# The projection weights of the stick-breaking layer: split in the second FFN stage, kept in DRAM as halves, and loaded as halves

## The chip, the cores and the metric

The kernel runs on one core of one Trainium2 chip. The metric is the device time of one execution in microseconds (us). Engines are called PE (TensorE's matmuls; PEld its weight loads), DVE (VectorE), ACT (ScalarE), POOL (GpSimd) and SP (SyncE, whose queue issues nearly all DMAs).

## The reference

The network runs over 1024 tokens of width 1024, all in float32. In order: an FFN (SwiGLU, 1024 to 2816 to 1024), a token mixer with two kinds of softmax attention, a second FFN, a layer with a linear recurrence and a state-space scan (the even layer, on 1040 tokens: 16 meta tokens are put in front), and the stick-breaking layer (the odd layer), which the change is about:

```python
u = rmsnorm(h, norm_w)
q, k, v, g = jnp.split(u @ w_in, 4, axis=-1)          # w_in: 1024 x 4096
...                                                   # 16 heads of 64
z = einsum(q, k) * 64 ** -0.5
log_keep = where(before, log_sigmoid(-z), 0)
csum = cumsum(log_keep, axis=-1)
weights = where(before, exp(log_sigmoid(z) + csum[..., -1:] - csum), 0)
o = einsum(weights, v)
o = o * silu(g)
return h + o @ w_out
```

## The kernel before

**Exact products from halves.** Every operand of a large product is split into two halves of the type `F32R`: `hi`, a rounding copy made on ACT (`nc.scalar.copy`), and `lo = raw - hi`, made on DVE. A product is three matmuls (`mm3`, lines 336 to 338): hi by hi, hi by lo, lo by hi. Weights come from DRAM as they are ("raw") and are split in SBUF (`Stream.split`, line 473 for the subtraction; the cast has the line of a wrapper, 224).

**Stages.** Five stages follow one another: first FFN, mixer, second FFN, even layer, odd layer. In the profile below they begin at about 0, 640, 1330, 1990 and 2790 us. Inside a stage, the work is written as many small threads (Python generators). Each says before an instruction which engine it needs and how long it will take by the planner's own costs ("A" for ACT, "V" for DVE, "P" for PE, "D" for SP's queue), and waits for buffers (`Res`) and events (`Ev`). The planner `Sched` picks the thread that can start first, and among equals the one of the lower priority number; this sets the order of the instructions. The framework below it places semaphores and buffers, and lets an instruction pass others on its engine when its buffers are free: the first DMA of the thread `ahead_of` (below) leaves at 31.4 us, although the planner starts that thread behind products that PE reaches later.

**Weight units of the odd layer.** `odd_stage` (line 2150) takes the 4096 columns of `w_in` as 32 units of 128 x 1024 numbers (512 KB): for each of eight pairs of heads p one unit for q, k and g each (`Stream.cols`: 128 columns, all eight blocks of 128 rows), and for each two pairs two units for v. Their order is q, k, g, v, v for p = 0, then q, k, g for odd p and q, k, v, v, g for even p; the last is g of pair 7. `Stream.thread` (line 479) loads a unit into one of 2 raw tiles, waits for one of 3 pairs of buffers (`wh`, `wl`) and starts the split. The pair comes free when PE is done with the unit.

**The odd stage's order.** The projections (`proj`) are the lowest in priority and fill PE between the parts of the attention, which goes pair by pair: scores `psc`, two sigmoids on ACT (`kt`, `pt`), a scan on DVE (line 2235), a product on DVE (line 2239), transposes `ptr` on PE (line 1573), their split into `th` on ACT and `tl` on DVE (line 1524), and the matmuls `po` with v (line 1556). The result goes to DRAM (`ooD`). Then comes the output projection (`Attention.out_proj`, line 1638; matmuls `pwo`, lines 1696 to 1698): when the projections are done it loads the halves of `w_out` into the buffers Ah and Al that held the stage's input, and then, block by block of 128 tokens, the operands `or` from `ooD`, into raw tiles:

```python
for k in range(KD):
    for x in range(2):
        yield ("D", 1.6)
        nc.sync.dma_start(WO[x][:, k, :D].bitcast(F32), w_out[x, k])
    ...
for t in range(8):
    yield ready(0, t // 2)
    yield W.r_raw
    yield W.r_hl
    raw = W.raw("o")
```

**Halves made ahead.** For the output weights of the mixer and of the odd layer this is already done: `Stream.ahead_of` (line 507) loads a unit, splits it, and stores both halves to a DRAM tensor (`wo1` in the first FFN stage, `wo2` in the even stage; tiles `pre`, eight units each, both raw tiles for one unit). In an FFN stage the thread `halves_ahead` runs it with the lowest priority from the fourth block of the gate and up weights on. In the second FFN stage it does not run; its two raw tiles hold a meta row and two loads for the even layer.

Of the kernel before, what the change touches and what calls it, by code (L numbers as in the profile page):

```python
# [427 lines left out]

class Stream:
# [4 lines left out]
    def __init__(self, c, eng="V", pool=None, nraw=0, nhl=0, shared=True):  # L434
# [44 lines left out]
    def thread(self, items, prio=4):  # L479

        c = self.c
        for key, units in items:
            if key in self.w:
                continue
            parts = []
            for x, srcs in enumerate(units):
                srcs = srcs if isinstance(srcs, tuple) else (srcs,)
# [12 lines left out]
                t = yield DMA_IN  # L500
                c.sch.spawn(self.split(raw[:, :n], hi[:, :n], lo[:, :n], n,
                                       self.ev[key] if x == len(units) - 1 else None, self.eng), prio, t)
                v = lambda t: t[:, :n].rearrange("p (k f) -> p k f", k=m)
                parts.append((v(hi), v(lo)))
            self.w[key] = lambda k, parts=parts, m=m: (parts[k // m][0][:, k % m], parts[k // m][1][:, k % m])

    def ahead_of(self, w, dst):

        nc = self.c.nc
        for k in range(KD):  # L510
            yield self.r_raw
            yield self.r_raw
            raw, hi = self.raw("pre"), self.raw("pre", F32R)
            yield ("D", 1.6)
            nc.sync.dma_start(raw, w[k * P:k * P + P, :])
            yield DMA_IN
            yield ("A", act(1024))
            nc.scalar.copy(hi, raw)
            yield ("V", dve(1024))
            nc.vector.tensor_sub(raw.bitcast(F32R), raw, hi.bitcast(F32))  # L520
            yield 0.5
            yield ("D", 1.6)
            nc.sync.dma_start(dst[0, k], hi.bitcast(F32))
            yield ("D", 1.6)
            nc.sync.dma_start(dst[1, k], raw)
# [154 lines left out]
def ffn_stage(c, A, first, rows0, wg, wu, wd, gpost, res, rows, nxt, meta=None, cols=None, later=None):  # L680
# [13 lines left out]
    with ExitStack() as ctx:  # L694
# [621 lines left out]
        def halves_ahead():  # L1316
            yield event("prod", 3, 1, "g")
            yield from W.ahead_of(*later)
# [31 lines left out]
class Attention:  # L1350
# [3 lines left out]
    def __init__(self, c, ctx, A, w_in, col0, psb, np_, nth, lo_eng):  # L1354
# [6 lines left out]
        self.W = Stream(c, lo_eng)  # L1361
# [276 lines left out]
    def out_proj(self, oD, w_out, after, ready, evac, last=KD - 1):  # L1638
# [10 lines left out]
        def load():  # L1649
            yield after  # L1650
            WO.extend(c.new_A())
            for k in range(KD):
                for x in range(2):
                    yield ("D", 1.6)
                    nc.sync.dma_start(WO[x][:, k, :D].bitcast(F32), w_out[x, k])
# [78 lines left out]
def mixer_stage(c, A, rows0, prm, w_in, forget_b, lams, subln, rope, w_out, gpost, res, rows):  # L1734
# [3 lines left out]
    with ExitStack() as ctx:  # L1738
        T = Attention(c, ctx, A, w_in, 0, dict(sc=3, tr=2, po=1, mm=2), 6, 2, "V")
# [410 lines left out]
def odd_stage(c, A, rows0, prm, w_in, w_out, res, final, out):  # L2150
# [3 lines left out]
    with ExitStack() as ctx:  # L2154
        T = Attention(c, ctx, A, w_in, M, dict(sc=3, tr=2, po=1, mm=2), 6, 2, "V")
# [5 lines left out]
        order = []  # L2161
        for p in range(8):
            order += [(p, "q"), (p, "k")] + ([(p, "g"), (p, "v")] if p == 0 else [(p, "v"), (p, "g")] if p % 2 == 0
                                             else [(p, "g")])
        items = [(j, Stream.cols(w_in, "qkvg".index(j[1]) * D + j[0] * P, 256 if j[1] == "v" else P)) for j in order]
        for key, _ in items:
            W.expect(key)
# [291 lines left out]
def even_stage(c, A, rows0, prm, w_in, lru_wa, lru_wx, dt_bias, a_log, ssd_d, w_out, meta, res, rows, later):  # L2459
# [701 lines left out]
    def weights():  # L3161
        yield from W2.into(w_out, D, WO[0], WO[1], ev_wl, 2, "V")
        yield from W2.ahead_of(*later)
# [15 lines left out]
def kernel(ctx, tc, x, ffn1_pre_g, ffn1_post_g, ffn1_w_gate, ffn1_w_up, ffn1_w_down, mix_pre_g, mix_post_g,  # L3179
# [19 lines left out]
    wo1, wo2 = (c.dr.tile([2, KD, P, D], F32, name=nm) for nm in ("wo1", "wo2"))  # L3199
# [6 lines left out]
                   later=(w_out[0], wo1))  # L3206
# [7 lines left out]
    def meta_rows(t, junk):  # L3214
# [15 lines left out]
    A4 = even_stage(c, A3, rows3, prm, even_w_in_2[0], lru_w_a_2[0], lru_w_x_2[0], ssd_dt_bias_2,  # L3230
                    ssd_a_log_2, ssd_d_2, even_w_out_2[0], meta_2, x3, rows4, (odd_w_out_2[0], wo2))
    odd_stage(c, A4, rows4, prm, odd_w_in_2[0], wo2, h1,
# [36 lines left out]
```

## Time and profile before

| | |
|---|---|
| median of 3 runs | 3589.42 us (3587.85 to 3590.59) |
| the profiled execution | 3594.18 us, of which span 3592.5 us |
| PE, DVE, ACT, POOL busy | 96%, 77%, 47%, 9% of the span |
| granted PE clock, mean | 0.987 |
| DMA traffic | 366.07 MB, mean 102 GB/s |
| HBM read, written | 267.58 MB, 95.13 MB |

"Busy" is the time in which an engine executes; matmuls are pipelined, so the bars of neighbouring matmuls overlap and the busy time of PE says that it is fed, not that it is at its peak. Times of rows count from the start of the span. `x<-y` names the tile that an instruction writes and those that it reads. "Idle before" is time in which the engine stood still in front of an instruction, with what ended it. A thing on "the chain" is a piece of the path that ended last, followed back from the end.

### The profile page before, as it was taken

To read this page: it belongs to the slowest core of one execution; us is meant where nothing else is said; L and a number is where in the kernel's file an instruction comes from. 1 tells how busy PE (TensorE), PEld (TensorE's weight loads), DVE (VectorE), ACT (ScalarE), POOL (GpSimd) and SP (SyncE) were. 2 spreads that over 40 slices of the span, in tenths; PEclk is the share of its full clock that TensorE was granted. 3 is DMA by queue.
4 is the path that set the end of the run, shared out by engine and by line. 5 is a ranking of instruction groups with operands and counts; after the bars stand their busy time and mean duration, and the time that the engine had idled before them with its cause. 6 is when DMAs were issued, how large, how long until landed. Compare 5 with 4: busy or idle time off the path is not lost.

```text
span 3592.5 us, 51852 instructions
## 1 busy us (share of the span) xinstructions
PE 3434.7 (96%) x19675; PEld 2929.4 (82%) x19675; DVE 2763.9 (77%) x5074; ACT 1696.3 (47%) x3451; POOL 328.0 (9%) x355
## 2 busy tenths in 40 slices
PE   8899999899999999999999899998999999999998
PEld 6688888778888877888888899988878888888877
DVE  8877689988888769766799779578633788788784
ACT  4333244556666543233345447447422565556551
POOL 0111144000000001111351000000000000000000
PEclk9999999999999999999999999999999999999999
DMA  5452382321211551323562334244473110111133
GB/s 168 146 174 91 103 289 86 123 61 44 67 43 39 178 167 61 122 88 108 178 212 67 111 63 86 61 87 89 139 241 94 57 36 22 39 30 30 34 134 107
DMA packets 305842, 366.07 MB, mean 102 GB/s; under 512 B 18644, under 2 KB 221568, under 8 KB 305592
## 3 DMA queue, kind: packets, MB, share of 16 engines
q1 hardware_dynamic: 299800, 341.71, 30.6%
q10 hardware_dynamic: 5792, 21.04, 1.6%
q8 instruction: 155, 2.54, 0.3%
q14 instruction: 95, 0.78, 0.1%
HBM read 267.58 MB, written 95.13 MB: 101 GB/s over the span
## 4 chain that ended last, share of the span: by engine, by line
PE 71%; DVE 19%; ACT 5%; issue 3%; DMA 2%; SPq 0%; POOL 0%; ACTq 0%; DVEq 0%; POOLq 0%
PE pst L338 7%; PE pst L337 7%; PE pst L336 7%; PE po L1556 3%; PE pe L336 3%; PE pe L338 3%; PE pe L337 3%; DVE kt L2235 3%; PE pdn L337 2%; PE pdn L338 2%; PE pdn L336 2%; PE ptr L1573 2%; DVE dl L1073 2%; PE pwo L3060 2%; PE pwo L3061 2%
## 5 line engine op out<-in xcount | busy, mean ns | idle before, releaser
L336 PE MATMUL pe<-Ah,wh 128*128 128x260 f32 (+1 forms) x1184 | 341.2, 289 | 19.9 <-DVE sz L2561 7.9
L338 PE MATMUL pe<-Ah,wl 128*128 128x260 f32 (+1 forms) x1184 | 337.8, 286 | 0.0
L337 PE MATMUL pe<-Al,wh 128*128 128x260 f32 (+1 forms) x1184 | 337.1, 285 | 0.0
L224 ACT CAST wh<-w 128x512 fp32r<-128x512 f32 x280 | 161.8, 619 | 225.3 <-PE pst L337 137.8
L338 PE MATMUL pst<-Ah,wl 128*128 128x512 f32 x640 | 253.3, 397 | 11.8 <-DVE wl L473 11.8
L916 DVE TENSOR_TENSOR sg<-sg,pst 128x512 f32<-128x512 f32 x280 | 185.9, 680 | 98.4 <-PE pst L338 98.1
L980 POOL TENSOR_TENSOR h<-h 128x512 f32<-128x512 f32 x88 | 137.2, 1560 | 1339.4 <-DVE h L962 1334.3
L337 PE MATMUL pst<-Al,wh 128*128 128x512 f32 x640 | 255.1, 399 | 0.0
L336 PE MATMUL pst<-Ah,wh 128*128 128x512 f32 x640 | 253.9, 397 | 1.2 <-DVE sg L916 1.2
L1524 DVE TENSOR_TENSOR tl<-ptr,th 128x512 fp32r<-128x512 f32 (+2 forms) x344 | 198.6, 591 | 63.9 <-ACT th L224 61.2
L473 DVE TENSOR_TENSOR wl<-w,wh 128x512 fp32r<-128x512 f32 x280 | 211.6, 782 | 44.7 <-ACT wh L224 43.4
L336 PEld LDWEIGHTS pe<-Ah,wh 128*128 128x128 f32 (+1 forms) x1184 | 224.1, 189 | 24.3 <-DVE sz L2561 8.2
L224 ACT CAST th<-ptr 128x512 fp32r<-128x512 f32 (+2 forms) x344 | 171.2, 515 | 147.2 <-PE ptr L1573 137.7
L337 PE MATMUL pdn<-dl,dh 128*128 128x512 f32 x592 | 230.8, 390 | 2.3 <-DVE dl L1073 2.3
L338 PE MATMUL pdn<-dh,dl 128*128 128x512 f32 x592 | 230.3, 389 | 0.0
L336 PE MATMUL pdn<-dh 128*128 128x512 f32 x592 | 229.0, 389 | 0.0
L337 PEld LDWEIGHTS pe<-Al,wh 128*128 128x128 f32 (+1 forms) x1184 | 223.6, 189 | 1.0
L338 PEld LDWEIGHTS pe<-Ah,wl 128*128 128x128 f32 (+1 forms) x1184 | 223.5, 189 | 0.8
L2235 DVE TENSOR_TENSOR_SCAN kt<-kt,onec 128x392 f32<-128x392 f32 (+6 forms) x224 | 202.5, 913 | 25.4 <-ACT kt L224 24.1
L224 ACT CAST wh<-wr 128x1024 fp32r<-128x1024 f32 (+2 forms) x116 | 119.3, 1028 | 167.8 <-PE pwo L3061 75.9
L336 PE MATMUL pst<-T,wh 128*128 128x512 f32 x480 | 187.6, 391 | 2.8 <-ACT T L224 2.8
L338 PE MATMUL pst<-T,wl 128*128 128x512 f32 x480 | 186.7, 390 | 1.1 <-DVE wl L473 1.1
(552 smaller groups left out, 10103.4 us busy)
## 6 DMA issues: line engine op xcount, KB each, us to landing
hD<-h SPq DMA_DIRECT2D x22, 1792.0 KB, 6.2
w<-in_ffn_w_gate_dram SPq DMA_DIRECT2D x20, 1024.0 KB, 5.5
w<-in_ffn_w_up_dram SPq DMA_DIRECT2D x20, 1024.0 KB, 7.8
d<-hD SPq DMA_DIRECT2D x18, 1024.0 KB, 5.5
wr<-in_even_w_in_dram SPq DMA_DIRECT2D x36, 512.0 KB, 4.6
wo<-prer SPq DMA_DIRECT2D x32, 512.0 KB, 3.2
wr<-in_odd_w_in_dram SPq DMA_DIRECT2D x32, 512.0 KB, 4.2
wr<-in_w_in_dram SPq DMA_DIRECT2D x24, 512.0 KB, 3.9
```

What stands on the lines that cost most here:

```text
L224: self.last = _o(*a, **k)
L336: nc.tensor.matmul(ps, wh, xh, start=start, stop=False)
L337: nc.tensor.matmul(ps, wh, xl, start=False, stop=False)
L338: nc.tensor.matmul(ps, wl, xh, start=False, stop=stop)
L473: (nc.gpsimd if eng == "G" else nc.vector).tensor_sub(lo, raw, hi.bitcast(F32))
L916: nc.vector.tensor_add(dst, src, ps)
L980: nc.gpsimd.tensor_sub(q[:, o], q[:, a], q[:, b_])
L1073: nc.vector.tensor_sub(lo, v[:, r], hi.bitcast(F32))
L1524: nc.vector.tensor_sub(tl[:rows, :n], ptr[:rows, :n], th[:rows, :n].bitcast(F32))
L1556: nc.tensor.matmul(po[:, 256 - n:256], vs, (th, tl)[which][:rows, o:o + n], start=(x == 0 and y == 0), stop=(x == last and y == len(lhs) - 1))
L1573: nc.tensor.transpose(ptr[:rows, o:o + P], pts[i][:, col:col + rows], c.ident)
L2235: nc.vector.tensor_tensor_scan(rev, rev, c.one.to_broadcast([P, m]), kt[:, k0 + m:k0 + m + 1], op0=ALU.mult, op1=ALU.mult)
```

## The change

The second FFN stage gets a list of 32 units to make ahead (`later=odd_u`): it loads each unit of the odd layer's `w_in` in the layout in which the odd stage will use it, casts it on ACT, subtracts on DVE, and stores both halves to a DRAM tensor `wio` (32 units, two halves each, 32 MB). The odd stage loads both halves of a unit by two DMAs, directly into a pair (`wh`, `wl`), and casts and subtracts nothing. Its two raw tiles become a fourth pair, until the projections are done; then `give_raw` returns them to the output projection. The output weights use the same class `Halves`, with no change in what is done for them.

```diff
+class Halves:
+    def __init__(self, src, dst):
+        self.src, self.dst, self.shape = src, dst, src.shape
+        self.n = src.shape[1] * src.shape[2]
+    @staticmethod
+    def of(c, name, items):
+        n = sum(len(us) for _, us in items)
+        dst = c.dr.tile([n, 2, P, 1024], F32, name=name)
...
 class Stream:
+        if halves:
+            self.hls.append((None, 0))
-        self.r_raw, self.r_hl = Res(len(self.raws)), Res(len(self.hls))
+        self.r_raw, self.r_hl = Res(0 if halves else len(self.raws)), Res(len(self.hls))
...
     def hl(self, name):
         pool, n = self.hls[self.ihl % len(self.hls)]
         self.ihl += 1
+        if pool is None:
+            return self.raw(name, F32R), self.raw(name, F32R)
...
+    def give_raw(self):
+        if self.hls[-1][0] is None:
+            yield self.r_hl
+            self.hls.pop()
+            for _ in range(len(self.raws)):
+                self.r_raw.release(self.c.sch.time)
...
     def thread(self, items, prio=4):
+                if isinstance(srcs, Halves):
+                    m, n = srcs.shape[1], srcs.n
+                    yield self.r_hl
+                    hl = [h[:, :n] for h in self.hl("w")]
+                    for y, h in enumerate(hl):
+                        t = yield ("D", 0.2 + 1.4e-3 * n)
+                        c.nc.sync.dma_start(h.bitcast(F32), srcs.dst[y, :, :n])
...
-    def ahead_of(self, w, dst):
+    def ahead_of(self, units):
-        for k in range(KD):
+        for u in units:
+            n = u.n
             yield self.r_raw
             yield self.r_raw
-            raw, hi = self.raw("pre"), self.raw("pre", F32R)
+            raw, hi = self.raw("pre")[:, :n], self.raw("pre", F32R)[:, :n]
-            nc.sync.dma_start(raw, w[k * P:k * P + P, :])
+            nc.sync.dma_start(raw.rearrange("p (k f) -> p k f", k=u.shape[1]), u.src)
             yield DMA_IN
             nc.scalar.copy(hi, raw)
             nc.vector.tensor_sub(raw.bitcast(F32R), raw, hi.bitcast(F32))
             yield 0.5
-            nc.sync.dma_start(dst[0, k], hi.bitcast(F32))
-            nc.sync.dma_start(dst[1, k], raw)
+            for x, h in enumerate((hi.bitcast(F32), raw)):
+                yield ("D", 0.2 + 1.4e-3 * n)
+                nc.sync.dma_start(u.dst[x, :, :n], h)
...
     def out_proj(self, oD, w_out, after, ready, evac, last=KD - 1):
             yield after
+            yield from W.give_raw()
             WO.extend(c.new_A())
...
+    odd, odd_u = Halves.of(c, "wio", odd_weights(odd_w_in_2[0]))
     A3 = ffn_stage(c, A2, False, rows2, ffn2_w_gate[0], ffn2_w_up[0], ffn2_w_down[0], ffn2_post_g, x2,
-                   rows3, even_weights(even_w_in_2[0], lru_w_a_2[0], lru_w_x_2[0])[:NXT], meta_rows)
+                   rows3, even_weights(even_w_in_2[0], lru_w_a_2[0], lru_w_x_2[0])[:NXT], meta_rows,
+                   later=odd_u)
```

## Rows read from the trace of the kernel before

**Rows 1.** The page: busy time, share of the span and instructions of each engine.
```profile
PE 3434.7 (96%) x19675; PEld 2929.4 (82%) x19675; DVE 2763.9 (77%) x5074; ACT 1696.3 (47%) x3451; POOL 328.0 (9%) x355
```

**Rows 2.** Busy time by stretch (stretch, length, then each engine), odd stage.
```profile
2780.00:3440.00 660.00, 618.23 (x4200) 547.32 (x4199) 518.01 (x914) 374.51 (x901) 16.97 (x132) 0.99 0.12 35
```

**Rows 3.** Line 1556, 2830 to 3440 us: what ended its idle time (us, times).
```profile
  DVE tl L1524: 70.9, 84
```

**Rows 4.** The chain, 2780 to 3440 us: start, us, what.
```profile
2787.58 1.05 ACT wh L224
...
2820.14 1.20 DVE wl L473
...
3339.79 1.06 ACT wh L224
3340.87 1.23 DVE wl L473
```

**Rows 5.** Busy time by stretch, first and second FFN stage (PE, PEld, DVE, ACT, POOL, clock, DMA).
```profile
138.00:212.00 74.00, 74.00 (x323) 60.46 (x322) 59.74 (x90) 27.77 (x46) 10.44 (x5) 1.00 0.61 215
...
1375.00:1450.00 75.00, 69.89 (x298) 55.55 (x297) 71.58 (x107) 25.11 (x44) 12.89 (x8) 0.98 0.31 102
1450.00:1550.00 100.00, 100.00 (x436) 81.62 (x436) 69.12 (x106) 31.25 (x56) 17.80 (x12) 1.00 0.29 98
```

**Rows 6.** Tile wr, 2800 us to the end: ns min/median/max, first and last start.
```profile
L224 ACT CAST wh<-wr x29: 1042/1049/1137, 2818.6 to 3408.0; 128x1024 fp32r<-128x1024 f32 x29
L473 DVE TENSOR_TENSOR wl<-wr,wh x29: 1189/1216/1226, 2820.1 to 3409.1; 128x1024 fp32r<-128x1024 f32 x29
```

**Rows 7.** DMA issues of the whole kernel: count, KB each, median us to landing.
```profile
wr<-in_odd_w_in_dram SPq DMA_DIRECT2D x32, 512.0 KB, 4.2
...
Al<-wo SPq DMA_DIRECT2D x16, 512.0 KB, 10.7
```

**Rows 8.** Waits of SP's queue, 2740 us to the end: total, times, longest.
```profile
SPq L496 <- DVE wl L473: 339.7, 25, 42.6
```

**Rows 9.** Timeline of SP's queue at the end of the odd stage: start, us, instruction.
```profile
3407.23 3.51 SPq L1674 DMA_DIRECT2D or<-ooD  x2
...
3463.48 0.32 SPq L1655 DMA_DIRECT2D Ah<-wo  x1
...
3483.33 0.39 SPq L1674 DMA_DIRECT2D or<-ooD  x1
```

**Rows 10.** Tile pg (gates), 3400 us to the end: the last matmul's start.
```profile
L338 PE MATMUL pg<-Ah,wl x28: 389/394/400, 3400.2 to 3463.0; 128*128 128x512 f32 x28
```

**Rows 11.** Tile pwo (output projection), 3440 us to the end: first and last start.
```profile
L1696 PE MATMUL pwo<-Ah,oh x128: 387/394/477, 3469.6 to 3582.4; 128*128 128x512 f32 x128
```

**Rows 12.** Busy time by stretch, instructions on tile pwo alone.
```profile
3464.00:3495.00 31.00, 10.32 (x36) 6.31 (x36) 0.00 (x0) 0.00 (x0) 1.00 0.79 292
```

**Rows 13.** Busy time by stretch, all instructions, the end of the odd stage.
```profile
3464.00:3495.00 31.00, 27.62 (x162) 20.82 (x161) 30.24 (x53) 19.20 (x48) 0.49 (x5) 1.00 0.79 292
3495.00:3584.00 89.00, 88.29 (x412) 72.16 (x412) 47.81 (x133) 19.87 (x37) 0.00 (x0) 1.00 0.34 110
```

**Rows 14.** Tile prer (units made ahead), 130 to 215 us: ns min/median/max.
```profile
L520 DVE TENSOR_TENSOR prer<-prer x7: 1210/1224/1226, 138.7 to 209.1; 128x1024 fp32r<-128x1024 f32 x7
...
L224 ACT CAST prer<-prer x6: 1048/1053/1055, 144.6 to 207.4; 128x1024 fp32r<-128x1024 f32 x6
```

**Rows 15.** Timeline of SP's queue, 138 to 216 us: loads of units made ahead.
```profile
140.41 0.38 SPq L515 DMA_DIRECT2D prer<-in_w_out_dram  x1
...
187.23 1.66 SPq L515 DMA_DIRECT2D prer<-in_w_out_dram  x1
...
203.03 0.37 SPq L515 DMA_DIRECT2D prer<-in_w_out_dram  x1
```

**Rows 16.** Timeline of SP's queue, 1285 to 1400 us: a raw tile is taken again.
```profile
1385.39 0.37 SPq L496 DMA_DIRECT2D wr<-in_even_w_in_dram  x1
```

**Rows 17.** Busy time by stretch, the down projection of the second FFN stage.
```profile
1770.00:1981.00 211.00, 209.82 (x925) 172.98 (x923) 203.40 (x266) 107.90 (x197) 79.00 (x37) 1.00 0.49 169
```

More of the change, by code (lines that the diff above doesn't have):

```diff
@@ L426, with place, __init__ @@
 DMA_IN = 2.4
+class Halves:
[6 more added lines that the diff above has]
+        dst = c.dr.tile([n, 2, P, 1024], F32, name=name)
+        units = []
+        def place(u):
+            units.append(Halves(u, dst[len(units)]))
+            return units[-1]
+        return [(key, [place(u) for u in us]) for key, us in items], units
 class Stream:
     RAW, HL = 2, 3
-    def __init__(self, c, eng="V", pool=None, nraw=0, nhl=0, shared=True):
+    def __init__(self, c, eng="V", pool=None, nraw=0, nhl=0, shared=True, halves=False):
         self.c, self.eng = c, eng
@@ L486, in thread @@
             for x, srcs in enumerate(units):
+                if isinstance(srcs, Halves):
[5 more added lines that the diff above has]
+                        c.nc.sync.dma_start(h.bitcast(F32), srcs.dst[y, :, :n])
+                    if x == len(units) - 1:
+                        self.ev[key].set(t + DMA_IN)
+                    parts.append([h.rearrange("p (k f) -> p k f", k=m) for h in hl])
+                    continue
                 srcs = srcs if isinstance(srcs, tuple) else (srcs,)
@@ L1317, in halves_ahead @@
             yield event("prod", 3, 1, "g")
-            yield from W.ahead_of(*later)
+            yield from W.ahead_of(later)
         def begin():
@@ L1350, with __init__ @@
 class Attention:
-    def __init__(self, c, ctx, A, w_in, col0, psb, np_, nth, lo_eng):
+    def __init__(self, c, ctx, A, w_in, col0, psb, np_, nth, lo_eng, halves):
         self.c, self.A, self.w_in, self.col0 = c, A, w_in, col0
@@ L1360, in __init__ @@
         self.pq, self.pv, self.pp, self.pm = opn("aQ"), opn("aV"), opn("aP"), opn("aM")
-        self.W = Stream(c, lo_eng)
+        self.W = Stream(c, lo_eng, halves=halves)
         self.np, self.nth = np_, nth
@@ L2145, in mixer_stage, with odd_weights, odd_stage @@
     return nA[0]
-def odd_stage(c, A, rows0, prm, w_in, w_out, res, final, out):
+def odd_weights(w_in):
+    order = []
+    for p in range(8):
+        order += [(p, "q"), (p, "k")] + ([(p, "g"), (p, "v")] if p == 0 else [(p, "v"), (p, "g")] if p % 2 == 0
+                                         else [(p, "g")])
+    return [(j, Stream.cols(w_in, "qkvg".index(j[1]) * D + j[0] * P, 256 if j[1] == "v" else P)) for j in order]
+def odd_stage(c, A, rows0, prm, w_in, items, w_out, res, final, out):
     nc, tc, sch = c.nc, c.tc, c.sch
@@ L2154, in odd_stage @@
     with ExitStack() as ctx:
-        T = Attention(c, ctx, A, w_in, M, dict(sc=3, tr=2, po=1, mm=2), 6, 2, "V")
+        T = Attention(c, ctx, A, w_in, M, dict(sc=3, tr=2, po=1, mm=2), 6, 2, "V", True)
         T.identb = prm["identb"]
@@ L2160, in odd_stage @@
         gts = {}
[L2161 to L2166, printed above, removed]
+        order = [key for key, _ in items]
+        for key in order:
             W.expect(key)
@@ L3162, in weights @@
         yield from W2.into(w_out, D, WO[0], WO[1], ev_wl, 2, "V")
-        yield from W2.ahead_of(*later)
+        yield from W2.ahead_of(later)
     sch.spawn(weights(), 2)
@@ L3197 @@
     x1, x2, x3, h1 = (rows_of(nm) for nm in ("x1", "x2", "x3", "h1"))
-    wo1, wo2 = (c.dr.tile([2, KD, P, D], F32, name=nm) for nm in ("wo1", "wo2"))
+    rows_w = lambda w: [("o", [w.rearrange("(k p) f -> p k f", p=P)[:, k:k + 1] for k in range(KD)])]
+    wo1, wo2 = (Halves.of(c, nm, rows_w(w))[1] for nm, w in (("wo1", w_out[0]), ("wo2", odd_w_out_2[0])))
     A = c.new_A()
@@ L3205 @@
                    x[0], rows1, mixer_weights(w_in[0])[:NXT], cols=cols,
-                   later=(w_out[0], wo1))
+                   later=wo1)
     rows2 = Rows(c, prm["g2"], x2, 0, 0)
```

16 lines of the change are left out of this document (7 added, 9 removed).

## The prediction

> **What bounds the kernel now.** I began with the page's busy line: TensorE (PE) is busy for 96% of the span, VectorE (DVE) for 77% [rows 1]. That is a mean over five stages, so next came the table of busy time by stretch for the last stage, the stick-breaking layer, whose weights the change moves. From 2780 to 3440 us PE is busy 618.2 of 660 us, DVE 518.0 and ScalarE (ACT) 374.5 [rows 2]: 41.8 us are left in which PE does nothing. The answer for line 1556 says what it waits for: weight loads and matmuls of that line sat 70.9 us, in 84 waits, for `tl`, a DVE result [rows 3] (a wait of a weight load and of its matmul overlap, so this counts parts twice). So the stage is a PE stage with holes, and the holes are DVE's. The chain of waits shows which DVE work is ahead of them: among its longest pieces from 2780 to 3440 us stand six casts `wh` on ACT (first at 2787.58, last at 3339.79) and eleven subtractions `wl` on DVE (first at 2820.14, last at 3340.87) [rows 4]. These are the splits of the projection weights.
>
> The second FFN stage, which gets the work, looks different: between 1450 and 1550 us PE is busy all 100 us, DVE only 69.1 and ACT 31.3 [rows 5].
>
> **The change part by part.** *Removed from the last stage:* 32 casts and 32 subtractions, one of each per weight unit. 29 of them fall behind 2800 us, at a median of 1.049 us and 1.216 us [rows 6]; 32 x 1.05 = 34 us of ACT, 32 x 1.22 = 39 us of DVE. What counts is the part on the path: 11 x 1.2 + 6 x 1.05 = 13.1 + 6.3 = 19.4 us [rows 4]. That is the most this chain can give. The least is nothing: the next chain, through the scans and `tl` themselves, may end just as late. I take half, 10 us: six of the eleven subtractions stand alone on the chain (some 7 us that only push other DVE work back), while five come as a pair behind a cast that itself waited for PE to free a buffer, and there a part of the wait stays.
>
> The Trainium skill would have this at nothing: "Perfetto Trace Analysis", section "Identifying the Most-Contended Engine", says in my words that the engine with the highest occupancy is the one to relieve, and that is PE here. By that rule this term is 0 and the sum is 10 us higher; it is weighed with the rivals.
>
> *Loads in place of splits.* Each unit now needs two 512 KB loads where it had one, straight into the buffers that the matmuls read. A raw load landed in 4.2 us (median), low halves of `wo`, loaded in bursts of sixteen, in 10.7 us [rows 7]; the split took 1.05 + 1.22 us with its load done beforehand. So a unit is ready some 2 to 8 us later after a buffer comes free. Against that stands a fourth pair of buffers (the two raw tiles). The first q, k and g of the stage use buffers that PE frees one after another before it needs them. I cost this at 0, for behind 2800 us no DMA is among the long pieces of the chain; without that cover it would be those 2 to 8 us for each unit that PE reaches early. SP's queue waits for these loads already: 339.7 us in all, 25 times, for a subtraction to free a raw tile [rows 8]; now it waits for PE to free a buffer. Behind them in the queue stand the `ooD` stores, and DVE's join of two heads waits for the two buffers that they free; one kind of wait in that queue takes the place of another of the same number, so I cost this at 0 too.
>
> *The end of the last stage.* The last weight unit (gate columns of head pair 7) is number 32 of 32, and 32 is a multiple of four, so it lies in the raw pair. Before, both raw tiles were free early: the first loads of the output projection's operands, `or<-ooD`, left at 3407.23 us [rows 9]. Now they can leave only when the last gate matmul is done, which starts at 3463.0 us [rows 10]. At that moment the 16 loads of the output weights `Ah/Al<-wo` become free to go too (from 3463.48), and they stand ahead in the order of the stage; the next `or` load behind them left at 3483.33 [rows 9]. SP's queue holds these, and behind them the later `or` loads and the `ooD` stores. So I expect the first operand to be loaded behind 8 MB, split by about 3495 us, and the matmuls `pwo`, which started at 3469.6 us [rows 11], to start some 25 us later. In 3464 to 3495 us they are 36 matmuls and 10.3 us of PE's busy time [rows 12]; at 100 / 436 = 0.23 us a matmul, as where PE is never idle [rows 5], that is 8.3 us. PE cannot fill the hole with attention, since DVE is busy 30.2 of these 31 us, nor catch up, since from 3495 us on it is busy 88.3 of 89 us [rows 13]. Cost: 0 (if the operands still come first) to 10.3 us; I take 8, the row it is nearest to being the 36 matmuls at their spacing.
>
> *Added to the second FFN stage:* 32 units of load, cast, subtraction and two stores. The first FFN stage has eight such units for the first output weights, so their price can be read: a cast takes 1.05, a subtraction 1.22 us [rows 14]. Six of them lie in 138 to 212 us, where DVE rises to 59.7 of 74 us (81%) and the DMA engines to 61%, and PE is still busy 74.00 of 74.00 us [rows 5]. So one unit in about 12 us costs PE nothing there. 32 of them add 39 us of DVE and 48 MB of traffic to a stage that has 31% of DVE free while it makes gate and up. SP's queue gets 96 more DMAs; behind their waits stand the loads of gate and up weights, as in the first stage, where PE saw nothing of it.
>
> The question is whether they are done in time. Two raw tiles allow one unit at once. From load to load the first stage took (203.03 - 140.41) / 5 = 12.5 us, at most 15.8 [rows 15]. The raw tiles are both free from 1385.39 us [rows 16], and the down projection begins at about 1770 us; 32 x 12.5 = 400 us ends at 1786 us, one or two units late. In the down projection DVE is busy 203.4 of 211 us [rows 17], so a unit there costs up to its 1.22 us. I take 1 us (two units less what the free 7.6 us swallow); bounds 0, and 7.7 units x 1.22 = 9.4 us at the slowest spacing.
>
> **Sum.** -10 + 8 + 1 = -1 us. Against the profiled execution's own 3594.18 us (span 3592.5 and 1.7 around it) that is 3593.2; this execution stands 4.8 us above the median of 3589.42, so the forecast is 3588 us: no change that can be measured. A change within 0.2% (7.2 us) is what a measurement of this kernel cannot tell from none.
>
> **Rivals.**
> *Faster: the holes close.* If the whole 19.4 us of splits come off the chain and the new order of the stage loads the first `or` operands early enough for half of the 8 us, the sum is -19.4 + 4 + 1 = -14: 3575 us. For it: PE's 41.8 us of holes are twice that, and they follow DVE. Against it: scans and `tl`, not the splits, are most of DVE's time there.
>
> *Slower: the late output projection alone decides.* Its place is 3464 to 3495 us, its price 8.3 to 10.3 us. If the relief of DVE gives less than about 2 us, because PE's own work sets the stage (it is busy 94% of it [rows 2]) and another DVE operation is late in the place of `wl`, the sum is 0 + 9 + 1 = +10: 3599 us. The rule of the Trainium skill named above leads to this case; the 70.9 us of waits for `tl` speak against it.
>
> *Slower: the units reach the down projection.* At 15.8 us each they end at 1385 + 506 = 1891 us; 7.7 units lie behind 1770 us, in front of `dl`, the operand that PE waits for there. With the other terms as forecast: -10 + 8 + 9.4 = +7.4, or 3597 us. It decides from a spacing of about 13 us on. For it: DVE is nearly full from 1375 to 1450 us (71.6 of 75 [rows 5]), so the first units may be slow. Against it: the trace shows idle DVE and ACT to fill.
>
> **How the numbers follow.** No measurable change 0.42, the holes close 0.32, the output projection alone 0.14, spill 0.12. Both slower cases lie above 7.2 us, so faster 0.32, same 0.42, slower 0.26. The range takes the faster case in, down to the bounds of -19.4 + 0 + 1 (3571), and both slower ones with some of what lies above them: 3571 to 3602 us. The likeliest case alone reaches from 3582 to 3596.
>
> **What would show it.** Right: no `wl<-wr` or `wh<-wr` behind the last even-layer operand; PE's busy time in the last stage up to `pwo` shorter by some 10 us for the same matmuls; the first `or<-ooD` load behind the last gate matmul and `pwo` starting 30 us behind it instead of 7; PE in the second FFN stage still at 100% until the down projection, with 32 subtractions `pre` at 1.2 us about 12 us apart. Wrong: the wait of line 1556 for `tl` unchanged (the term of -10), an `or` load ahead of the `wo` loads (the +8), `pre` operations behind 1800 us or holes of PE beside gate and up weights (the +1), or a wait of PE for a load from the new DRAM tensor (the 0).

## The result and the profile after

The changed kernel takes 3670.13 us (median of 4 runs, 3663.43 to 3673.99) against 3589.72 us: ratio 1.022, 95% interval 1.0205 to 1.0236. It is slower by 80 us, where no measurable change was forecast. The page's busy line, which answers to [rows 1]:

```profile
PE 3454.6 (94%) x19675; PEld 2946.1 (80%) x19675; DVE 2771.2 (75%) x5074; ACT 1694.9 (46%) x3451; POOL 344.2 (9%) x355
```

The matmuls are the same 19675. PE's busy time grows by 19.9 us and the span by 79.8, so most of the loss is holes. To find their places, the start of the same matmul (same tile name, same number among that tile's matmuls) is compared in the two traces, from each span's start. The table gives how many us later than in the kernel before the landmark starts; the runs below stand in the same columns. The first row is the landmark's time before. The columns: the 17th gate or up matmul `pst` of the second FFN stage (just ahead of the blocks in question), the first down matmul of that stage, the first `pe` matmul of the even stage, its first `psd`, its last `pe`, the last gate matmul `pg` of the odd stage, the last matmul.

```
                 pst    down    pe   psd  last pe  last pg  last pwo
before (us)   1378.6  1769.8 1995.2 2050.7 2578.0  3463.0   3582.9
after           -1.7    18.9   21.7   65.8   66.2    68.3     79.8
e1 make only    -1.4    13.8   16.6   59.6   60.1    56.9     56.9
e2 load only    -0.5    -0.6   -0.8   -2.0   -0.8    -0.3     10.8
e3 load, tail   -0.3    -0.3   -0.5   -1.7   -0.9    -1.1      1.2
e4 prefetch     -2.7    23.7   40.2   39.6   41.5    43.4     54.8
e5 same order   -3.3    -3.4   -3.7   -4.0   -3.8    -4.5     -4.5
e6 late cast    -2.9     7.2    7.0  118.8  120.5   117.9    117.9
e7 small store  -1.8    18.0   17.8   48.7   51.8    48.7     48.7
e8 make 8        0.1     1.0    1.0    0.8    2.6    -0.2     -0.1
e9 pool cast     2.2    26.0   28.5   83.6   84.6    81.2     81.3
e10 pool store  -3.0    42.3   42.1   88.4   89.5    87.1     87.1
e11 pool both   -1.2    46.5   46.5  106.4  108.3   104.7    104.7
e12 make 22     -2.4    11.7   13.0   12.4   15.0    11.5     11.6
e13 paced 20     2.0     3.7   15.1   15.1   16.3    14.7     15.1
```

Equal code differs between two traces by up to 10 us where PE waits (18.9, 13.8 and 23.7 in the `down` column come from the same instructions), and the profiled execution of before is 4.8 us above its median, so the offsets at the end read 1 to 10 us lower than differences of medians.

So the loss has three places: 20.6 us in gate and up, 44.1 us at the head of the even stage, 11.5 us behind the last gate. The middle of the odd stage, where 10 us were to be won, lost 2. It is more when held against the nine runs below that keep the old odd stage (e1, e6 to e13): between last `pe` and last `pg` they are 1.6 to 3.6 us faster than this one trace of the kernel before.

*Gate and up.* Busy time by stretch, to be held against [rows 5]:

```profile
1450.00:1550.00 100.00, 99.97 (x435) 81.30 (x435) 71.38 (x104) 32.31 (x53) 16.07 (x8) 1.00 0.61 202
1550.00:1650.00 100.00, 95.15 (x403) 76.15 (x402) 74.01 (x102) 34.18 (x57) 23.73 (x12) 0.98 0.60 197
1650.00:1770.00 120.00, 113.53 (x481) 90.50 (x480) 87.82 (x125) 40.63 (x69) 21.69 (x12) 0.99 0.60 196
```

For 100 us PE stays full, as the prediction had it, with DMA at 0.61; then holes open, though DVE and ACT are far from full. From 1450 to 1770 us PE's weight loads wait for split weights, and DVE, in a step ahead of the splits, for the loads of up weights (total us, times, longest):

```profile
DVE w L828 <- DMA w<-in_ffn_w_up_dram: 17.8, 7, 3.7
PEld pst L338 <- DVE wl L505: 11.3, 8, 1.6
PEld pst L336 <- ACT wh L224: 5.7, 5, 1.9
```

In the kernel before, PE was busy for all 320 us of that stretch. There the gate load waited for its own buffer (first line). In the changed kernel it hardly does (second line), and SP stands in front of the stores of the units instead (third line):

```profile
SPq L736 <- DVE wl L473: 54.8, 6, 9.3
SPq L779 <- DVE wl L505: 6.3, 12, 0.9
SPq L568 <- ACT prer L224: 165.3, 21, 10.3
```

SP's queue shows a round, the DMAs from the gate load of one block of weights to that of the next (start, us, instruction):

```profile
1533.32 0.38 SPq L779 DMA_DIRECT2D w<-in_ffn_w_gate_dram  x1
...
1534.56 1.50 SPq L559 DMA_DIRECT2D prer<-in_odd_w_in_dram  x1
1544.89 4.17 SPq L568 DMA_DIRECT2D wio<-prer  x2
1549.16 0.38 SPq L559 DMA_DIRECT2D prer<-in_odd_w_in_dram  x1
1555.05 1.74 SPq L568 DMA_DIRECT2D wio<-prer  x2
1563.00 0.37 SPq L1025 DMA_DIRECT2D hD<-h  x1
1563.48 0.51 SPq L559 DMA_DIRECT2D prer<-in_odd_w_in_dram  x1
1572.83 1.59 SPq L568 DMA_DIRECT2D wio<-prer  x2
1575.29 0.38 SPq L779 DMA_DIRECT2D w<-in_ffn_w_gate_dram  x1
```

Three units stand in each round, and each is load, wait for the cast, store, wait for the subtraction, store. From the gate load at 1488.8 to the one at 1703.3 us five rounds take 42.9 us each; in the kernel before, 38.4 (1480.14 to 1672.06). ACT's timeline shows the same from the other side: the cast waits 10.71 us for its load, and four weight casts stand behind it.

```profile
1571.76 1.05 ACT L224 CAST prer<-prer 128x1024 fp32r<-128x1024 f32 x1 [10.71 <-DMA prer<-in_odd_w_in_dram]
1572.71 2.17 ACT L224 CAST wh<-w 128x512 fp32r<-128x512 f32 x4
```

*Head of the even stage.* SP's queue again, 1725 to 2120 us (x5 joins five loads):

```profile
1732.68 0.50 SPq L559 DMA_DIRECT2D prer<-in_odd_w_in_dram  x1
1745.91 3.20 SPq L539 DMA_DIRECT2D wr<-in_even_w_in_dram  x2
1989.15 0.38 SPq L539 DMA_DIRECT2D wr<-in_even_w_in_dram  x1
2009.98 0.38 SPq L559 DMA_DIRECT2D prer<-in_odd_w_in_dram  x1
...
2088.02 0.38 SPq L559 DMA_DIRECT2D prer<-in_odd_w_in_dram  x1
2096.25 12.95 SPq L539 DMA_DIRECT2D wr<-in_even_w_in_dram  x5
```

23 units are made by 1744 us. Then the prefetch of the even stage takes both raw tiles, which come free only when the even weights' buffers do, about 2000 us. The other nine units run from 2009.98 us on, one by one, and the next even weights wait behind them until 2096.25. PE waited 34.0 us at once for the cast of an even weight, and the mean granted clock of the stretch was 0.74:

```profile
2003.00:2110.00 107.00, 59.16 (x410) 54.53 (x411) 58.47 (x88) 41.86 (x69) 1.66 (x14) 0.74 0.57 193
```

The same 410 matmuls took 62.9 us in the kernel before (1981.3 to 2044.2 us, clock 0.92).

*Odd stage.* First the stretch that answers to [rows 2], then what ended the idle time of the line in [rows 3]:

```profile
2845.00:3505.00 660.00, 615.61 (x4181) 548.55 (x4179) 482.81 (x880) 345.54 (x868) 17.65 (x132) 0.99 0.17 58
```

```profile
  DVE tl L1567: 57.4, 88
  ACT th L224: 14.8, 15
  ACT pt L224: 4.1, 3
  DVE oo L1635: 3.6, 3
```

DVE has 35 us less to do, ACT 29, the wait for `tl` is 13.5 us shorter, and PE does not run denser: 615.6 of 660 us.

*Tail.* The last gate matmul, the first and last `pwo`, and SP's queue between them ([rows 9 to 11]):

```profile
L338 PE MATMUL pg<-Ah,wr x16: 389/394/403, 3514.2 to 3531.4; 128*128 128x512 f32 x16
```

```profile
L1740 PE MATMUL pwo<-Ah,oh x128: 388/394/483, 3570.2 to 3662.2; 128*128 128x512 f32 x128
```

```profile
3531.55 0.32 SPq L1699 DMA_DIRECT2D Al<-wo  x1
...
3535.33 0.52 SPq L1699 DMA_DIRECT2D Ah<-wo  x1
3548.29 0.32 SPq L2333 DMA_DIRECT2D ooD<-oo  x1
...
3552.17 3.15 SPq L1718 DMA_DIRECT2D or<-ooD  x2
```

### The profile page after: what moved, and what is told of

The parts are those of the page before. It is cut to its first block, busy times and chain, and to the rows that moved or that the text cites. A ratio compares the mean times of both kernels' runs of the same rounds, so it can differ in the third digit from the quotient of the medians.

```text
span 3672.3 us, 52100 instructions
## 1 busy us (share of the span) xinstructions
PE 3454.6 (94%) x19675; PEld 2946.1 (80%) x19675; DVE 2771.2 (75%) x5074; ACT 1694.9 (46%) x3451; POOL 344.2 (9%) x355
## 4 chain that ended last, share of the span: by engine, by line
PE 63%; DVE 19%; DMA 7%; ACT 5%; issue 3%; POOL 2%; SPq 1%; DVEq 0%; ACTq 0%; POOLq 0%
PE pst L338 4%; PE pst L337 4%; PE pst L336 4%; PE po L1599 3%; PE pdn L337 3%; PE pdn L338 3%; PE pdn L336 3%; DMA prer<-in_odd_w_in_dram 3%; PE pe L336 3%; PE pe L338 3%; PE pe L337 3%; DVE kt L2284 3%; PE ptr L1616 2%; POOL h L1023 2%; PE pwo L3109 2%
## 5 line engine op out<-in xcount | busy, mean ns | idle before, releaser
L1023 POOL TENSOR_TENSOR h<-h 128x512 f32<-128x512 f32 x88 | 151.4, 1721 | 1352.9 <-DVE h L1005 1347.7
L505 DVE TENSOR_TENSOR wl<-w,wh 128x512 fp32r<-128x512 f32 x280 | 221.2, 818 | 22.6 <-ACT wh L224 22.0
L2284 DVE TENSOR_TENSOR_SCAN kt<-kt,onec 128x392 f32<-128x392 f32 (+5 forms) x224 | 202.9, 915 | 34.4 <-ACT kt L224 33.5
L336 PE MATMUL pst<-T,wh 128*128 128x512 f32 x480 | 188.6, 393 | 3.8 <-ACT T L224 3.8
L337 PE MATMUL pst<-T,wh 128*128 128x512 f32 x480 | 188.7, 394 | 0.0
```

The source lines that it names most:

```text
L336: nc.tensor.matmul(ps, wh, xh, start=start, stop=False)
L337: nc.tensor.matmul(ps, wh, xl, start=False, stop=False)
L505: (nc.gpsimd if eng == "G" else nc.vector).tensor_sub(lo, raw, hi.bitcast(F32))
L1023: nc.gpsimd.tensor_sub(q[:, o], q[:, a], q[:, b_])
L2284: nc.vector.tensor_tensor_scan(rev, rev, c.one.to_broadcast([P, m]), kt[:, k0 + m:k0 + m + 1], op0=ALU.mult, op1=ALU.mult)
```

## The experiments

**The two halves of the change (e1, e2).** e1 makes the units and reads the raw weights as before; e2 makes nothing and reads, in their place, the halves of the output weights that the first FFN stage stored (other values, same sizes). e3 and e5 read these too.

```diff
 # e1
-T = Attention(c, ctx, A, w_in, M, dict(sc=3, tr=2, po=1, mm=2), 6, 2, "V", True)
+T = Attention(c, ctx, A, w_in, M, dict(sc=3, tr=2, po=1, mm=2), 6, 2, "V", False)
-odd_stage(c, A4, rows4, prm, odd_w_in_2[0], odd, wo2, h1,
+odd_stage(c, A4, rows4, prm, odd_w_in_2[0], odd_weights(odd_w_in_2[0]), wo2, h1,
 # e2: no later=odd_u; the units of odd are
+        odd[-1][1].append(Halves(u, wo1[i % KD].dst))
```

> Only the making is kept: the second FFN stage makes and stores the 32 units as in the changed kernel, but the odd stage loads the raw projection weights and splits them as in the kernel before, so the stored halves are read by nobody. Theory A (the loss is made in two places ahead of the odd stage: 20.6 us in the gate and up matmuls of the second FFN stage and 44 us at the head of the even stage, by the offsets of equal matmuls between the two traces): 3589.7 + 65 = about 3655 us (3648 to 3662), the odd stage as long as in the kernel before. Theory B (what the prediction held: making is hidden under the FFN stage, the loss comes from reading the halves in the odd stage): 3588 to 3595 us.

> Only the reading is kept: nothing is made in the second FFN stage, and the odd stage loads its weights as pairs of halves, from the halves of the output weights that the first FFN stage has stored long before (other values, same shapes, sizes and instructions). Theory A: no cost ahead of the odd stage, about +11.5 us at the output projection, and 0 to -6 us in the middle of the odd stage: 3595 to 3602 us. Theory B: the odd stage holds most of the loss, 3640 us or more. The prediction's own terms, -10 for the splits and +8 for the late operand loads, would make 3588 us; offsets tell which of the two terms is off.

e1: 3653.36 us, ratio 1.0173 (1.0158 to 1.0188). e2: 3605.71 us, 1.0041 (1.0026 to 1.0056). Theory A holds: 64 of the 80 us are made ahead of the odd stage, by work that nobody reads, and with the 16 of e2 the two halves add up to the whole. e2 is 4 us above A's range: its tail lost 11 us by the offsets, and its middle is some 4 us slower, not faster, when held against e1, which has the old odd stage (-3.2 us from last `pe` to last `pg`, e2 +0.5).

**The tail (e3).** The raw pair leaves the rotation three units earlier.

```diff
                 if isinstance(srcs, Halves):
                     m, n = srcs.shape[1], srcs.n
+                    if key == (7, "q"):
+                        yield from self.give_raw()
```

> As the run that only reads (weights from the first FFN stage's stored halves, nothing made), but the pair of raw tiles leaves the rotation of weight pairs before the last three units (query, key and gate of the last head pair), so that the operand loads of the output projection need not wait for the last gate. Theory A (the late raw pair makes the whole loss of the tail): the first output matmul comes some 7 us after the last gate matmul instead of 38, and the run is 10 to 12 us below the one that only reads, 3584 to 3590 us. Rival C (the queue of SP, stalled on the store of the last attention output, or the loads of the output weights behind it make the loss): within 3 us of the run that only reads.

3596.37 us, 1.0020 (1.0011 to 1.0029): 9.3 us below e2. The last gate matmul starts at 3461.9 us, the first `pwo` at:

```profile
L1742 PE MATMUL pwo<-Ah,oh x128: 388/394/483, 3471.6 to 3583.6; 128*128 128x512 f32 x128
```

10 us behind it instead of 39. The mechanism of the tail is shown; rival C falls. The total misses the expected 3584 to 3590, as what is left above the kernel before (7 us, 1.1 to 2.9 per mille) is in neither theory.

**The relief of DVE by itself (e5).** The planner is told that the splits are still there, so the order stays the old one and only the work is gone.

```diff
                 if isinstance(srcs, Halves):
                     m, n = srcs.shape[1], srcs.n
+                    yield self.r_raw
+                    yield ("D", 0.2 + 1.4e-3 * n)
                     yield self.r_hl
                     hl = [h[:, :n] for h in self.hl("w")]
...
+                    t = yield DMA_IN
+                    c.sch.spawn(self.no_split(n, self.ev[key] if x == len(units) - 1 else None), prio, t)
```

> Nothing is made in the second FFN stage; the odd stage loads pairs of halves (of the output weights stored by the first FFN stage: other values, same sizes) in place of raw weights, but the planner is told the costs of the raw load and of the split all the same, and the three pairs rotate as before. So the order of all other work, and the tail, is that of the kernel before, and only the 32 casts and subtractions of the odd stage are gone. In the run that only reads, the middle of the odd stage gained nothing although VectorE had 35 us and ScalarE 29 us less to do. Theory M (the new order that the planner made, with four pairs in rotation, ate a gain that is there): about the 10 us of the prediction come back, 3576 to 3584 us. Theory P (TensorE bounds the stage and its waits only change their names): 3585 to 3593 us, with the waits of po for tl down by about 6 us and others up.

3589.70 us against 3590.16, ratio 0.9996 (0.9987 to 1.0005): theory P. The interval leaves at most 4.7 us of gain, so 10 are excluded. The run takes the relief and the loads in place of the splits together; its trace lists no wait of PE or of its weight loads for a DMA in the odd stage, so nothing shows the loads hiding a gain. The stretch of [rows 2], moved to the same matmuls, and the waits of [rows 3]'s line:

```profile
2775.50:3435.50 660.00, 619.18 (x4194) 549.07 (x4193) 486.43 (x884) 347.49 (x871) 17.09 (x132) 0.99 0.17 60
```

```profile
  DVE tl L1575: 65.6, 83
  ACT th L224: 13.9, 23
```

31.6 us of DVE and 27 us of ACT are gone, and PE gets 1 us. The wait for `tl` was not only a queue at DVE: over the whole run DVE itself stood idle before `tl` for 73.3 us because ACT's `th` was late, up from 61.2 us in the kernel before, and in the odd stage `th` in turn waited 91.4 us for PE's `ptr`, up from 84.8. It is a chain from PE's `ptr` over `th` and `tl` back to `po`; with less in DVE's queue it waits at `th` instead. e3 and e5 differ by 6.7 us with the same halves read: the four-pair rotation and the new order cost, they did not hide a gain. Which wait makes these 7 us is open.

**Nine units in front of the even weights (e4, e12).** e4 is the whole change with the even prefetch held back until the last unit; e12 makes 22 units, and none is left over.

```diff
 # e4
             yield event("op", 2, 3, 3)
+            if later and not first:
+                yield event("made")
             yield from ahead.thread(nxt, 2)
...
+            event("made").set(sch.time)        # behind the last unit
 # e12, on e1
-                   later=odd_u)
+                   later=odd_u[:22])
```

> The changed kernel whole, with one thing moved: the even stage's weights are prefetched only when the last of the 32 units is made, so they no longer take the two raw tiles while 9 units are still to be made. Theory A (the 44 us at the head of the even stage are those 9 units, made one after another in front of the even weights): the last units are made during the down projection, the head of the even stage is as in the kernel before, 3670 - 44 = 3626 us (3618 to 3634). Rival D (the 9 units cost the same wherever they stand, in the down projection or by making the even weights late): 3655 us or more. In between (3634 to 3655): the units cost part of it on the engines of the down projection, as the prediction's rival with 1.22 us a unit has it, 9 x 1.22 = 11 us.

> As the run that only makes, but the first 22 units alone, all of which stand before the down projection's loads on SP, three to a block of gate and up weights. Theory S (SP serves its queue in order; three units at 14.3 us make a block's round 43 us where TensorE needs 38.6, and a block's lead is soon used up): the gate and up matmuls lose as in the run that only makes, 14 to 24 us, and the head of the even stage nothing: 3604 to 3614 us.

e4: 3648.01 us (1.0142 to 1.0177), the case "in between": the loss at the head of the even stage is gone (40.2 to 39.6 in the table), but 16.5 us are lost in the down projection, where five of the nine units start behind its first matmul (1868.8 to 1920.9 us): about 3 us each and not 1.22. PE's longest wait in that stretch is for DVE's `dl`, 9.6 us where it was 1.2 in the kernel before. e12: 3611.20 us (1.0045 to 1.0079): 14 us lost by the first down matmul from its own start, none at the even stage. Both show that the 44 us are the nine units in front of the even weights.

**Why gate and up slow down (e6 to e11, e13).** All on e1, so nothing reads the halves. e6 tells the planner a landing of 10 us for a unit's load; e7 stores one eighth of each half's columns; e8 makes 8 units; e9 casts on GpSimd; e10 issues the stores from GpSimd; e11 does both.

```diff
 # e6
-            yield DMA_IN
+            yield late          # 10.0 in the second FFN stage
 # e7
-                nc.sync.dma_start(u.dst[x, :, :n], h)
+                nc.sync.dma_start(u.dst[x, :, :n // part], h[:, :n // part])   # part = 8
 # e8
-                   later=odd_u)
+                   later=odd_u[:8])
 # e9
...
-            nc.scalar.copy(hi, raw)
+            nc.gpsimd.tensor_copy(hi, raw) if pool else nc.scalar.copy(hi, raw)
 # e10
-                nc.sync.dma_start(u.dst[x, :, :n], h)
+                (nc.gpsimd if pool else nc.sync).dma_start(u.dst[x, :, :n], h)
```

> The second FFN stage makes all units, nobody reads them (as in the run that only makes), and the planner is told that a unit's load lands after 10 us instead of 2.4, so that its cast is put later in ScalarE's order. 15 units then come before the down projection's loads instead of 23 and 17 stand before the even stage's weights instead of 9, so the head of the even stage should lose about 44 x 17 / 9 = 83 us. The question is the gate and up matmuls, which lost 14 to 24 us with 23 units. Theory Q (casts planned too early block ScalarE's queue while their load is under way, and the weight casts behind them come late): under 5 us by the first down matmul, total 3589 + 83 + 4 = 3676 us. Theory T (the traffic of the units slows the gate and up weights): in proportion to the units, 14 to 24 x 15 / 23 = 9 to 16 us, total 3681 to 3692 us.

> As the run that only makes (nobody reads the halves), but each store of a half in the second FFN stage writes one eighth of its columns: a unit then moves 0.63 MB instead of 1.5, with the same instructions, waits and order. Theory T (traffic): by the first down matmul the loss falls from 14 to 24 us to under 8, and the head of the even stage gets shorter too, as each of its 9 units needs less. Theory Q (queues: casts that wait for their load on ScalarE, stores that wait for casts on SP): 12 us or more still lost by the first down matmul, and the 44 us at the head of the even stage stay within 10.

> As the run that only makes, but the first 8 units alone, which is as many as the first FFN stage makes. All 8 come before the down projection's loads, so the head of the even stage is as in the kernel before. The prediction's step (the units are hidden, since the 8 of the first FFN stage were): 3589 to 3591 us. Cost by the unit (14 to 24 us for 23 units, so 0.6 to 1.0 us each): 3594 to 3598 us. If the loss comes only where the unit's loads run into other traffic late in the stage, nothing is seen by the first down matmul.

> As the run that only makes (nobody reads the halves), but in the second FFN stage the cast of a unit stands on GpSimd instead of ScalarE, so that a cast that waits for its load holds up nothing on ScalarE; GpSimd is busy 16 us in 100 there. Loads, stores and their queue are as before; 22 units come before the even stage's weights instead of 23. Theory Q1 (the loss in the gate and up matmuls is the weight casts that stand behind a waiting unit's cast on ScalarE): at most 4 us lost by the first down matmul instead of 14 to 24. Theory Q2 (it is SP's queue: stores that wait for casts, with the gate and up loads behind them): still 12 us or more. Rival R (GpSimd's own work for the down projection, behind which the stores of h stand, comes late): the loss is not smaller, and DVE's waits for h grow. The head of the even stage loses 44 us or more in all cases.

> As the run that only makes, but the stores of the halves are issued from GpSimd's queue instead of SP's, so that no load stands behind a store that waits for its cast; the casts stay on ScalarE. Theory Q1 (ScalarE's queue): by the first down matmul 10 us or more still lost, unless the unit's loads land sooner because SP issues them sooner, which shows in ScalarE's waits for them (102 us in the run that only makes). Theory Q2 (SP's queue): at most 4 us lost there. The head of the even stage still loses some 40 us.

> Both: casts of the units on GpSimd and their stores issued from GpSimd. If either queue alone makes the loss, this is at most 4 us lost by the first down matmul; if it is the traffic of the units (1.5 MB each, 200 GB/s where the kernel before moves 100), it stays at 10 us or more.

Medians: e6 3711.01, e7 3644.44, e8 3593.88 (1.0004 to 1.0022), e9 3673.76, e10 3684.32, e11 3699.79 us. From `pst` to the first down matmul the four runs that make 22 or more units in one and the same way (after, e1, e4, e12) lost 14.1 to 26.4 us. None of the theories put on record for these runs came through whole:

- *Traffic (T).* e7 lost 19.8 us with 0.63 MB a unit instead of 1.5, and with 144 GB/s from 1550 to 1650 us where e1 has 203: not the traffic. (At the head of the even stage e7 lost 30.9 us and e1 43.0, so there the size of the stores counts.)
- *ScalarE's queue (Q, Q1).* e6 lost 10.1 us with 15 units, which is in T's range and not under Q's 5. e9 lost 23.8 us with ScalarE freed: not ScalarE's queue alone. Rival R, GpSimd's own work, has its sign against it, since DVE's waits for `h` went down, to 39.3 us from 51.4 in e1 (1375 to 1770 us).
- *Stores on SP that wait for casts (Q2).* e10 lost 45.3 us and e11 47.7 us with no store on SP, where at most 4 were expected. By that sign SP's queue fell too, in the form in which it was put. (The loss of e11 was to point to traffic, which e7 speaks against.)

e6 also lost 111.8 us at the even stage with 17 units (83 expected): those took 153 us there, nine in e1 85 us, and about 42 us of either stretch are covered.

What these runs share is a long round on SP, by the gate loads: 42.9 us after, 43.6 in e9 (1493.6 to 1711.5, five rounds), 44.2 in e7 (1489.8 to 1666.4, four; its units are shorter, but four fit into a round), 48.8 in e10 (1493.2 to 1688.3, four). In e10 SP no longer waits for casts, but its next load waits for the stores to free the raw tiles:

```profile
SPq L559 <- DMA wio<-prer: 151.1, 16, 12.4
```

There the gate load waits for its own buffer as well, 46.9 us in seven waits from 1450 to 1770 us: the splits that free the buffer stand behind the unit's cast and subtraction on ScalarE and VectorE (at 1587.46 us a cast had waited 8.2 us for its load, with four weight casts behind it). So in e10 SP's order is one part of the round, and those two queues are another.

e8 shows that a round may be late for a while. Its gate loads:

```profile
1488.90 0.38 SPq L779 DMA_DIRECT2D w<-in_ffn_w_gate_dram  x1
1533.26 0.38 SPq L779 DMA_DIRECT2D w<-in_ffn_w_gate_dram  x1
1568.84 0.37 SPq L779 DMA_DIRECT2D w<-in_ffn_w_gate_dram  x1
1603.88 0.37 SPq L779 DMA_DIRECT2D w<-in_ffn_w_gate_dram  x1
```

44.4 us with units in it, then 35.6 and 35.0. The second load stands 15.7 us behind its counterpart in the kernel before (1517.55 us), and by the first down matmul 0.9 us are lost: the weights are loaded some time ahead of their use, this lead covers such a delay, and it is filled up again. (The median of e8 is 3.7 us above that of the kernel before; the trace does not show where.) This gave theory S, in which SP serves its queue in order and the units make the round longer than PE's, and e13 to test it: at most two units a round, by a load that needs a number from the block's product.

```diff
+            for i, u in enumerate(later):        # later = odd_u[:20]
+                yield event("tick", i // 2)
+                yield from W.ahead_of([u], tick)
...
+                nc.vector.tensor_copy(raw[:, :1], tick)   # ahead of the unit's load
...
+                    nc.vector.tensor_copy(tick, q[:, 0, :1])   # when block b's h is done
```

> The first 20 units are made, nobody reads them, and two at most are let into each block's round: a unit's load waits for a number copied from the block's product h. 15 units stand before the down projection's loads and 5 between them. Theory S: two units at 14.3 us and the waits for h fit into TensorE's 38.6 us a block, so the gate loads come every 38.6 us and at most 3 us are lost by the first down matmul; total 3590 to 3597 us with what the 5 units cost in the down projection. Rival U (each unit has its price of 0.6 to 1.0 us by its work on ScalarE and VectorE and its traffic, wherever it stands): 15 units lose 9 to 15 us by the first down matmul, total 3601 to 3609 us. The 8 units alone, which lost 1 us there, fit both S (lead) and a threshold.

3612.57 us (1.0045 to 1.0075), but where the theories differ, S holds: with 17 unit loads issued before the first down matmul, 1.7 us are lost from `pst` to it, and PE is full:

```profile
1550.00:1650.00 100.00, 100.00 (x433) 81.03 (x432) 67.93 (x105) 30.27 (x52) 13.70 (x10) 1.00 0.52 181
1650.00:1770.00 120.00, 120.00 (x518) 97.05 (x517) 89.70 (x137) 39.07 (x68) 18.50 (x12) 1.00 0.47 173
```

Its rounds take 40.6 us (1479.85 to 1682.94, five), so they too use up lead, 2.2 us a round instead of 4.5. The last four units (loads from 1772.7 us on) cost 11.4 us in the down projection, again about 3 us each, and the total misses by that. A price for each unit wherever it stands (rival U) is out for gate and up.

The loss from `pst` to the first down matmul can be held against how late the last gate load is (us behind the 1672.06 of the kernel before):

```
       after   e1    e4    e6    e7    e8    e9   e10   e11   e12   e13
late    31.2  26.6  29.8  17.5  31.9   2.8  39.5  55.9  58.1  25.5  10.9
lost    20.6  15.2  26.4  10.1  19.8   0.9  23.8  45.3  47.7  14.1   1.7
```

The two go together, which fits a late round as what costs PE. What makes the round late is argued and not shown: SP's order fits after, e1, e7, e9 and e12, where the gate load hardly waits for its own buffer. But two units a round also put less in front of the splits on ScalarE and VectorE, so e13 does not tell SP's queue from theirs. A run with the units' loads and stores all on a queue of their own was not tried.

No version beats the kernel before: with reading alone the best is e5, equal to it, and every run that makes units adds to that.

## Why the prediction was wrong, step by step

- **The step that failed most: "I take 1 us", units made in time and nearly free.** Three of its parts were off. The spacing was 14.2 us (1447.9 to 1732.7 us, 20 units) and not 12.5, and the third unit only started at 1447.9. So nine were left at 1744 us, not one or two; the rival at 15.8 us a unit came near that count (7.7). Next, "behind their waits stand the loads of gate and up weights, as in the first stage, where PE saw nothing of it" carried a reading over six units to 32: eight cost 0.9 us there (e8), as the lead of the weight loads covers them; 23 cost 20.6 us. By e8, the six units of [rows 5, 15] were too few to use that lead up. Last, left-over units do not land in the down projection at 1.22 us each (there they would cost about 3: e4, e13), but behind the even prefetch that takes their two raw tiles: 44.1 us. The prediction named these tiles as the reason why one unit runs at a time, and [rows 16] even show an even weight taking one; it did not ask who takes them next.
- **The -10 us for the splits: nothing came.** e5 measures -0.5 us (-4.7 to +1.8) for this term and the loads in place of the splits together. The chain's 19.4 us [rows 4] were lengths of instructions that ended last there, not time that goes away with them. PE's holes follow DVE by name [rows 3], yet a chain of four engines' steps sets them. The rule weighed in the prediction, to relieve the engine of the highest occupancy ("Perfetto Trace Analysis" in the Trainium skill, section "Identifying the Most-Contended Engine"), gives 0 as the prediction applied it, and e5 agrees with that. The section names the engine to work on first, and judges TensorE by its use of peak rate and its share of weight loading (82% in [rows 1], still above DVE's 77%); what the relief of another engine is worth it does not say.
- **The +8 us for the late operand loads: right mechanism, size 11.5 us** (e3 takes 9.3 of it back). `pwo` started 39 us behind the last gate matmul, not 30: SP stood from 3535.8 to 3548.3 us for a store `ooD` between the weight loads, which I had left out.
- **Loads in place of splits at 0:** with the old order and three pairs that fits (e5, no wait of PE for a load). With the fourth pair and the new order the odd stage costs about 7 us (e3); which wait makes them is open.
- **The range** (3571 to 3602) could not hold it: its upper end took units at 9.4 us as the worst case, on the assumption that they delay nothing but DVE.

## What to carry to other kernels

Work moved into a "free" stretch takes a place in every in-order queue it passes: count its round on that queue (instructions, waits and landing times) against the round of the stage, and the lead that covers the difference, before pricing it by engine time. Ask of each buffer that it borrows who is the next to claim it, and what happens to the rest if that one comes first. Test a relief on the chip with the order held fixed: a wait that bears an engine's name may be a chain through that engine.

## What the runs showed of the hardware

The same chain of load, cast, subtraction and two stores took 14.2 us a unit beside gate and up, where its loads landed in 8.1 us (median), and 9.1 us at the head of the even stage in e6 (1995.3 to 2140.6 us, 17 units), where they landed in 2.7 us (3.3 us there in the changed kernel). In both places the core moved about 200 GB/s. In the changed kernel, while PE did little but wait for the even weights (2075 to 2107 us, busy 5.7 of 32 us), the mean granted clock was 0.53, close to the lower of its two levels (1.2 and 2.4 GHz); from 2110 to 2140 us, with PE at work again, it was 1.00.
